# Pool mixer, the next half layer's norm, three plain tiles and the first Strassen tile as one list of steps

## The chip, the cores and the metric

The kernel runs on one core of one Trainium2 chip. The metric is the device time of one execution in microseconds (us). Five engines of the core appear: PE (matrix multiply, with its weight loads shown as PEld), DVE (vector), ACT (scalar), POOL (GpSimd) and SP, which here only issues DMA transfers. Each engine works through its own instructions in order, and semaphores make one wait for another.

## The reference, cut to what matters

One step of a two-layer decoder on 512 prompt rows and 8 sample rows of width 1024. Each layer has two half layers of SwiGLU feed-forward with 2816 hidden columns and a mixer between them. Layer 0 mixes by causal pooling over windows of 2, 4, 8 and 16 rows, one window for each group of 256 columns; layer 1 by windowed attention with sinks.

```
for l in range(DEPTH):
    x = x + 0.5 * _swiglu(_rmsnorm(x, norm_g[l, 0]), ...)   # ffn 0 for l = 0
    h = _rmsnorm(x, norm_g[l, 1])
    if l < N_A_LAYERS:                                      # l = 0
        out, nbuf = _pool_mixer(h, pool_bufs[l], ...)       # (mean over the window - h) @ pool_w * scale
    else: ...                                               # attention
    x = x + out
    x = x + 0.5 * _swiglu(_rmsnorm(x, norm_g[l, 2]), ...)   # ffn 1 for l = 0
```

All of it is float32. `nbuf`, the last 15 mixer inputs, is an output too.

## The kernel before, in words

**Layout.** x is kept transposed: eight tiles `x[0..7]` of 128 columns of the model by 520 tokens (512 prompt, 8 sample). A float32 product is made of three matmuls on pairs: a high part and a low part of each operand (`xh`, `xl`; `wh`, `wl`), high by high, low by high, high by low. ACT makes the high part of a weight piece (L192), DVE the low part (L193). Raw weights come in chunks through SP's queue (L359) into three buffers.

**A half layer** (`ffn`, L683) makes 22 hidden tiles of 128 columns in parts of 8, 8 and 6, and adds each part's down-projection to x. A *plain* tile takes 96 matmuls of 260 columns (L519). A *Strassen* tile takes seven products of twelve matmuls (L545), 84 in all, and needs sums of blocks of x (`t1` to `t4`, L661 to L667, made once in a half layer) and sums of weight blocks, which POOL starts as accumulating DMAs (L156, L157) and DVE finishes (L162, L166). The first `NPL[fi]` tiles of half layer `fi` are plain, because the sums of x are not there yet; before, ffn 1 has two.

**Between ffn 0 and ffn 1.** The last down-projection gives x[0] to x[7] one after the other: u = result times R (L711), x updated (L712), its pair (L348, L349), its square added to `acc` (L468, L472). Then the mixer: `zt` multiplies the token blocks by `pool_w` (L1029, four groups of five blocks of six matmuls); the norm's sums are taken by ten small matmuls over `acc` (L483), the root by twelve small DVE operations (L491 to L498); the products are scaled by the root and split (`zt_evac`); `band` applies the window as a banded matrix, eleven matmuls of 256 columns and two of 8 for each m (L1054, L1062, L1063), and DVE adds the result to x, the 8 sample columns (L1064) apart from the 512 others (L1067). `hx` (L1077), turned by PE (L1097), is the last inputs' output. Then ffn 1 starts: its norm runs between the plain tiles' matmuls, and the sums of x are hooks called between them.

**Order.** Here the instructions of an engine stand in the order of the code, except that a scheduler may move some that are not kept (`later` keeps one). A class `Steps` (L237) exists and is used elsewhere: each step has an engine, a cost, a due time, the steps it must follow and the buffers it takes; `order` plays the engines forward and always starts the earliest-due step that is ready, and `emit` writes the instructions in that order.

SP's queue behind the chunks of weights holds, before ffn 1, one copy for the pooling state (L1107), two for the key and value windows (L1110), one load `sraw` (L1114) and sixteen of 64 bytes for `sink_s` (L1116); the loaded values are negated on DVE (L1147, L1149).

## Time and profile before

| | us |
|---|---|
| three timed runs, median | 1671.43 |
| lowest, highest | 1669.02, 1675.51 |
| the profiled execution | 1674.94 |
| its span in the trace | 1673.1 |
| PE busy | 1647.5 |
| DVE busy | 1254.4 |
| ACT busy | 884.6 |
| POOL busy | 175.2 |

A span reaches from the first to the last traced instruction. Matmul durations overlap, so PE's pace is read from the distance of two starts, or from a piece of the chain of waits with its count. Mean granted clock of PE over the span: 0.992 of full speed. In the prediction, "m6" and "m7" are the last two blocks of the down-projection of ffn 0, "z" the L1029 matmuls, "bands" the L1054 to L1063 matmuls, and times within the span are given as they stand in the trace of before.

### The profile page before, as it was taken

The page shows a single profiled execution, that of the slowest core. Times are in us where ns is not written, and L with a number is a line of the kernel's source. Part 1 is how long each engine was busy: PE and PEld are TensorE (multiplying, and loading weights), DVE is VectorE, ACT ScalarE, POOL GpSimd, SP SyncE. Part 2 cuts the span into 40 slices and gives each one's busy share as a digit, 9 for nine tenths or more (in the row PEclk, how much of TensorE's full clock was granted, in tenths as well). Part 3 has the DMA queues.
Part 4 walks back from the last instruction along what each step waited for, and adds up shares of the span by engine and source line. Part 5 has one row for each costly group of instructions (what it writes and reads, how often), then busy time and mean ns, then how long its engine had stood idle before and what let it go on. Part 6 is the DMA issues. An engine that isn't in the chain of part 4 may idle for free.

```text
span 1673.1 us, 34561 instructions
## 1 busy us (share of the span) xinstructions
PE 1647.5 (98%) x13802; PEld 1629.3 (97%) x13802; DVE 1254.4 (75%) x2400; ACT 884.6 (53%) x1763; POOL 175.2 (10%) x235
## 2 busy tenths in 40 slices
PE   9999999999899999999999999999999999999997
PEld 9999999999899999999999999999989999999997
DVE  7966866887785785878785785778987785785785
ACT  6643643656662562556562562555875663463463
POOL 1101101000101101100201110100220110110100
PEclk9999999999999999999999999999999999999999
DMA  9546846753466665633666666654142565675641
GB/s 241 133 132 135 182 132 136 175 161 97 93 162 152 139 162 145 142 108 114 154 157 156 135 154 162 139 147 113 27 102 71 112 160 143 141 171 137 141 115 52
DMA packets 318240, 227.08 MB, mean 136 GB/s; under 512 B 9568, under 2 KB 293336, under 8 KB 318038
## 3 DMA queue, kind: packets, MB, share of 16 engines
q1 hardware_dynamic: 291360, 178.50, 38.4%
q0 software_dynamic: 23392, 41.83, 15.5%
q10 hardware_dynamic: 3326, 4.53, 0.9%
q8 instruction: 108, 1.77, 0.4%
q14 instruction: 54, 0.44, 0.1%
HBM read 180.89 MB, written 5.04 MB: 111 GB/s over the span
## 4 chain that ended last, share of the span: by engine, by line
PE 93%; DVE 4%; ACT 1%; DMA 1%; issue 1%; DVEq 0%; ACTq 0%
PE ps L545 47%; PE ps L519 32%; PE pa L519 5%; PE ps L1780 2%; PE p L519 1%; PE pb L1385 1%; PE pc L1456 1%; PE ps L1029 1%; PE pc L1441 1%; DMA pr<-in_bands_dram 1%; PE ps L1054 1%; DVE wl L193 1%; PE ps L483 0%; PE t L809 0%; ACT wh L192 0%
## 5 line engine op out<-in xcount | busy, mean ns | idle before, releaser
L192 ACT ACTIVATE wh<-raw 128x512 fp32r<-128x512 f32 (+1 forms) x690 | 418.1, 622 | 511.4 <-PE ps L519 294.2
L193 DVE TENSOR_TENSOR wl<-raw,wh 128x512 fp32r<-128x512 f32 (+1 forms) x690 | 456.6, 677 | 193.1 <-ACT wh L192 189.5
L545 PE MATMUL ps<-th,wh 128*128 128x260 f32 x1264 | 358.5, 284 | 3.6 <-ACT th L345 1.7
L545 PE MATMUL ps<-tl,wh 128*128 128x260 f32 x1264 | 358.1, 284 | 0.6 <-DVE tl L346 0.6
L545 PE MATMUL ps<-th,wl 128*128 128x260 f32 x1264 | 356.4, 284 | 0.8 <-DVE wl L193 0.8
L545 PEld LDWEIGHTS ps<-th,wh 128*128 128x128 f32 x1264 | 238.9, 189 | 5.0 <-ACT th L345 2.1
L545 PEld LDWEIGHTS ps<-tl,wh 128*128 128x128 f32 x1264 | 239.3, 189 | 1.0 <-DVE tl L346 1.0
L545 PEld LDWEIGHTS ps<-th,wl 128*128 128x128 f32 x1264 | 238.4, 189 | 1.2 <-DVE wl L193 1.2
L519 PE MATMUL ps<-hh,wh 128*128 128x260 f32 x1024 | 206.6, 283 | 0.6 <-ACT vtok L1207 0.6
L519 PE MATMUL ps<-hl,wh 128*128 128x260 f32 x1024 | 207.1, 282 | 0.0
L519 PE MATMUL ps<-hh,wl 128*128 128x260 f32 x1024 | 205.1, 282 | 0.0
L545 PE MATMUL ps<-xh,wh 128*128 128x260 f32 x708 | 199.1, 284 | 2.0 <-ACT wh L192 1.5
L545 PE MATMUL ps<-xl,wh 128*128 128x260 f32 x708 | 198.7, 283 | 0.0
L157 POOL DMA_DIRECT2D raw<-raw x79 | 68.4, 866 | 1241.7 <-DVE wl L193 566.5
L545 PE MATMUL ps<-xh,wl 128*128 128x260 f32 x708 | 195.3, 283 | 1.4 <-DVE wl L193 1.4
L519 PEld LDWEIGHTS ps<-hl,wh 128*128 128x128 f32 x1024 | 158.4, 188 | 0.0
L519 PEld LDWEIGHTS ps<-hh,wh 128*128 128x128 f32 x1024 | 157.0, 188 | 1.0 <-ACT vtok L1207 0.9
L519 PEld LDWEIGHTS ps<-hh,wl 128*128 128x128 f32 x1024 | 157.4, 188 | 0.0
L545 PEld LDWEIGHTS ps<-xh,wh 128*128 128x128 f32 x708 | 133.7, 189 | 2.7 <-ACT wh L192 1.9
L711 DVE TENSOR_TENSOR u<-ps,R 128x520 f32<-128x520 f32 x88 | 61.3, 697 | 97.1 <-PE ps L519 97.1
L545 PEld LDWEIGHTS ps<-xl,wh 128*128 128x128 f32 x708 | 133.8, 189 | 0.0
L545 PEld LDWEIGHTS ps<-xh,wl 128*128 128x128 f32 x708 | 131.8, 189 | 1.8 <-DVE wl L193 1.8
(299 smaller groups left out, 3247.1 us busy)
## 6 DMA issues: line engine op xcount, KB each, us to landing
raw<-in_ffn_w_gate_dram SPq DMA_DIRECT2D x87, 512.0 KB
raw<-in_ffn_w_up_dram SPq DMA_DIRECT2D x87, 512.0 KB
raw<-in_ffn_w_down_dram SPq DMA_DIRECT2D x32, 1024.0 KB
S<-in_ffn_w_up_dram SPq DMA_DIRECT2D x79, 256.0 KB
raw<-raw POOLq DMA_DIRECT2D x79, 256.0 KB, 3.3
S<-raw POOLq DMA_DIRECT2D x79, 256.0 KB, 4.6
raw<-in_ffn_w_down_dram SPq DMA_DIRECT2D x16, 768.0 KB
raw<-in_w_q_dram SPq DMA_DIRECT2D x8, 512.0 KB
```

The source lines that it names most:

```text
L157: G.dma_start(blk(raw, 2, 1), blk(raw, 1, 1), accum_op=ALU.add)
L192: nc.scalar.activation(dh, src, AF.Copy)
L193: nc.vector.tensor_tensor(dl, src, dh.bitcast(F32), op=ALU.subtract)
L519: T.matmul(banks[:, hf, :H], a[:, kk, :], hcols(b, hf), start=(first and i == 0), stop=(last and i == 2),)
L545: T.matmul(bank[:, :H], a[:, kk, :], b, start=(not more and kk == 0 and i == 0), stop=(kk == 3 and i == 2), skip_group_check=more,)
L711: V.tensor_tensor(halves(u), banks[m][:, :, :H], halves(R), op=ALU.mult)
L1029: T.matmul(o, a[:, s], b[:, kk, :], start=(n == 0), stop=(n == 5))
L1054: T.matmul(po[:, half * 256 : half * 256 + 256], z[:, tau, c], b, start=(i == 0), stop=(i == len(lst) - 1),)
L1385: T.matmul(o, q_[rows_, qc], k_[rows_, kc_], start=(i == 0), stop=(i == 2))
L1441: T.transpose(pt[:, o : o + P], vals["sm", t, h, bi][:, e, kt * P : (kt + 1) * P], ident)
L1456: T.matmul(po[rows_, bi * P : (bi + 1) * P], vtok[:, max(b - 1, 0) + kt, v0 : v0 + 64], vals["pp", t, h, bi][:, kt * 256 + e * P : kt * 25 ...
L1780: T.matmul(bank, a[:, k % 3, :], b[:, c0:c1], start=(k == 0 and i == 0), stop=(k == 5 and i == 2))
```

## The change

`NPL` becomes (3, 3, 2, 2): ffn 1 has three plain tiles and one Strassen tile fewer. The last down-projection of ffn 0 stops after m = 5; its blocks m6 and m7, the mixer, its norm, ffn 1's norm, three plain tiles and the first six products of the first Strassen tile with the sums of x become one `Steps` list, which sets the order on PE, DVE, ACT and POOL. Further:

- The mixer's norm takes two matmuls for each block, one over `acc` (seven squares) and one over the last square; on PE these run as 20 instead of 10.
- Both norms' roots are one `pow` on POOL instead of the twelve operations on DVE.
- A band's result lies in columns 256 to 776 of a double bank, so that one DVE operation of 520 columns adds it to x.
- `hx` is copied before the norm is known, in pieces kept by the list; the first weight pieces of ffn 1 and the accumulating DMAs are steps too.
- The state, key and value copies, `sraw` and the sink loads are issued by SP one chunk of weights earlier.

```diff
-NPL = (3, 2, 2, 2)
+NPL = (3, 3, 2, 2)
...
-        ffn(0, tmp, mov0, first_hooks(), tt, HH, deferred(1, tmp, "g", XX, mov1, TW), pool_prep(), first_tile)
-
-    with tc.tile_pool(name="pm", bufs=2) as pm:
...
+        hs0 = ffn(0, tmp, mov0, first_hooks(), tt, HH, deferred(1, tmp, "g", XX, mov1, TW), pool_prep(), first_tile, stop=6)
+
+    movk, mov2, tt = [], [], {}
+    later(nc.sync.dma_start(pool_sample[0, :, 0:14, :], state_pool[0, :, 1:15, :]))
...
+    later(nc.sync.dma_start(sraw, attn_sinks.broadcast_to([P, 16])))
+    for b in range(16):
+        later(nc.sync.dma_start(sink_s[b * 8 : (b + 1) * 8, 4:6], attn_sinks.rearrange("l (g r) -> r (l g)", g=2)))
+    with ff_pool() as tmp:
+        first = W.ng
+        have = W.ns - first
+        st = Steps(dict(d=4, w=6, sb=4, sa=2, g=2, t=2, sq=2))
...
+        def norm_sums():
+            vals["f", 0] = f = duo()
+            for t in range(5):
+                lo = t * P if t < 4 else 400
+                o = f[:, 1, t : t + 1]
+                T.matmul(o, acc[:, lo : lo + P], ones[:, 0:1], start=True, stop=False)
+                T.matmul(o, vals["q", 1, 7][:, lo : lo + P], ones[:, 0:1], start=False, stop=True)
...
+        def norm_root():
+            nc.gpsimd.tensor_tensor(r_tok[:, :5], v, minus_half, op=ALU.pow)
...
+        def band(m, part):
...
+            if part == 0:
+                vals["b", m] = duo().rearrange("p a c -> p (a c)")
...
+            o = vals["b", m][:, 256 * part + 256 : min(256 * part + 512, 256 + TOK)]
...
-                V.scalar_tensor_tensor(
-                    x[m][:, SP:], pso[:, :NS], gcol(N_PS, m), x[m][:, SP:], op0=ALU.mult, op1=ALU.add
-                )
-                V.scalar_tensor_tensor(
-                    x[m][:, :SP], po, gcol(N_PS, m), x[m][:, :SP], op0=ALU.mult, op1=ALU.add
-                )
...
+        def x_out(m):
+            V.scalar_tensor_tensor(
+                x[m], vals["b", m][:, 256 : 256 + TOK], gcol(N_PS, m), x[m], op0=ALU.mult, op1=ALU.add
+            )
...
+        def mixed(hs):
+            out_hs.append(hs)
+            with tc.manual_schedule(
+                engines={mybir.EngineType.PE, mybir.EngineType.DVE, mybir.EngineType.Activation, mybir.EngineType.Pool}
+            ):
+                st.emit()
+            begun(1, 4)
+            return NP + 1
+
+        ffn(1, tmp, mov2, [], tt, HH, deferred(N_KV, tmp, "g", XX, movk), given=mixed)
```

**How the instructions move, place 1:** DVE at the end of ffn 0 (`x_82` is x[6], `x_83` x[7]; `raw_4505`, `raw_4645` and `raw_4651` are weight chunks of ffn 1's first tiles). Before:

```order
L193 TENSOR_TENSOR wl<-raw_4505,wh 128x512 [waits PE_49,Activation_49]
L711 TENSOR_TENSOR u<-ps_4817,R 128x520 [waits PE_49]
L349 SCALAR_TENSOR_TENSOR xl<-x_81,gT,xh 128x520 [waits Activation_49]
...
L349 SCALAR_TENSOR_TENSOR xl<-x_82,gT,xh 128x520 [waits Activation_49]
L711 TENSOR_TENSOR u<-ps_4818,R 128x520 [waits PE_49]
L472 TENSOR_TENSOR acc<-acc,sq 128x520 [waits Activation_49]
L346 TENSOR_TENSOR xl<-sts,xh 128x8 [waits Activation_49]
L193 TENSOR_TENSOR wl<-raw_4645,wh 128x512 [waits DMAHW2_49,Activation_49]
L712 SCALAR_TENSOR_TENSOR x_83<-u,x_83 128x520 [waits DVE_49]
L349 SCALAR_TENSOR_TENSOR xl<-x_83,gT,xh 128x520 [waits Activation_49]
```

After:

```order
L1308 TENSOR_TENSOR u<-ps_4874,R 128x520 [waits DVE_49,PE_49]
L1311 SCALAR_TENSOR_TENSOR x_82<-u,x_82 128x520 [waits DVE_49]
L225 TENSOR_TENSOR wl<-raw_4505,wh 128x512 [waits DMAHW6_49,Activation_49]
L1319 SCALAR_TENSOR_TENSOR xl<-x_82,gT,xh 128x520 [waits Activation_49]
L1337 TENSOR_TENSOR acc<-acc,sq 128x520 [waits Activation_49]
L1326 TENSOR_TENSOR xl<-sts,xh 128x8 [waits Activation_49]
L225 TENSOR_TENSOR wl<-raw_4505,wh 128x512 [waits Activation_49]
L1308 TENSOR_TENSOR u<-ps_4920,R 128x520 [waits PE_49]
L1311 SCALAR_TENSOR_TENSOR x_83<-u,x_83 128x520 [waits DVE_49]
L225 TENSOR_TENSOR wl<-raw_4505,wh 128x512 [waits Activation_49]
L1319 SCALAR_TENSOR_TENSOR xl<-x_83,gT,xh 128x520 [waits DVE_49,Activation_49]
```

The update of x[7] now stands right behind its u; before, three operations stood between them. The last square is no longer added to `acc` on DVE.

**Place 2:** SP behind the third chunk of ffn 1's weights. Before:

```order
L359 DMA raw_4770<-in_ffn_w_up_dram 128x8x128 [waits DMAHW4_49]
L359 DMA raw_4907<-in_ffn_w_gate_dram 128x8x128 [waits DMAHW6_49,DMAHW5_49,DVE_49]
L359 DMA raw_4907<-in_ffn_w_up_dram 128x8x128
L359 DMA S<-in_ffn_w_up_dram 128x4x128 [waits DMAHW7_49]
L1107 DMA out_dram<-in_state_pool_dram 8x14336 [waits DMAHW0_49]
```

After:

```order
L368 DMA raw_4796<-in_ffn_w_up_dram 128x8x128 [waits DMAHW4_49]
L1261 DMA out_dram<-in_state_pool_dram 8x14336 [waits DMAHW5_49]
L1264 DMA out_dram<-in_cache_k_win_dram 8x2x16256 [waits DMAHW6_49]
L1264 DMA out_dram<-in_cache_v_win_dram 8x2x16256 [waits DMAHW7_49]
L1268 DMA sraw<-in_attn_sinks_dram 128x16 [waits DMAHW0_49]
L1270 DMA sink_s<-in_attn_sinks_dram 8x2x1 [waits DMAHW1_49]
```

The copies and the small loads now stand ahead of the fourth chunk. The DVE operations that read the small loads (L1563 and L1565, formerly L1147 and L1149) move too, though the diff does not touch them. They now stand in the middle of the mixer's norm and its scaled products (L1350 is the mean, L1356 the fifth block's factor, L1392 the low parts of z); DVE after:

```order
L1326 TENSOR_TENSOR xl<-sts,xh 128x8 [waits Activation_49]
L1563 TENSOR_SCALAR nsinks<-sraw 128x8 [waits DMAHW0_49]
L1563 TENSOR_SCALAR nsinks<-sraw 128x8
L225 TENSOR_TENSOR wl<-raw_4651,wh 128x512 [waits DMAHW1_49,Activation_49]
L1350 TENSOR_SCALAR nv<-ps_5020 128x5 [waits PE_49]
L225 TENSOR_TENSOR wl<-raw_4651,wh 128x512 [waits DMAHW2_49,Activation_49]
L1356 TENSOR_SCALAR r_4869<-r_tok,sel 128x1 [waits Pool_49]
L1392 SCALAR_TENSOR_TENSOR hl<-ps_4974,r_tok,hh 128x256 [waits Activation_49]
L1392 SCALAR_TENSOR_TENSOR hl<-ps_4974,r_tok,hh 128x256 x3
L1565 TENSOR_SCALAR sink_s<-sink_s 128x2 [waits DMAHW4_49,DMAHW5_49,DMAHW3_49,DMAHW6_49,DMAHW2_49,DMAHW7_49,DMAHW1_49,DMAHW0_49]
L1565 TENSOR_SCALAR sink_s<-sink_s 128x2
L1392 SCALAR_TENSOR_TENSOR hl<-ps_5013,r_tok,hh 128x256 [waits Activation_49]
```

Before, they stood among the sums of x, 37 and 50 rows behind the last low part of z.

**Place 3:** DVE at the first Strassen tile (`t_...` are the sums of x, `tl` their low parts, `g` and `hl` a plain tile's result). Before:

```order
L193 TENSOR_TENSOR wl<-raw_4907,wh 128x512 [waits PE_49,Activation_49]
L561 TENSOR_TENSOR hl<-g,hh 128x520 [waits Activation_49]
L661 TENSOR_TENSOR t_5729<-xa 128x260
L662 SCALAR_TENSOR_TENSOR t_5729<-t_5729,xb 128x260 [waits DVE_49]
L667 SCALAR_TENSOR_TENSOR t_5730<-t_5729,xb 128x260 [waits DVE_49]
L346 TENSOR_TENSOR tl<-t_5729,th 128x520 [waits Activation_49]
L666 TENSOR_TENSOR t_5730<-xb,xa 128x260
L162 TENSOR_TENSOR raw_4907<-raw_4907,S 128x512 [waits DMASW2_49,DMASW1_49]
```

After:

```order
L163 TENSOR_TENSOR raw_5045<-raw_5045,S 128x512 [waits DMASW6_49]
L848 TENSOR_TENSOR tl<-t_5709,th 128x520
L848 TENSOR_TENSOR tl<-t_5636,th 128x520
L225 TENSOR_TENSOR wl<-raw_5045,wh 128x512 [waits PE_49,Activation_49]
L848 TENSOR_TENSOR tl<-t_5722,th 128x520
L225 TENSOR_TENSOR wl<-raw_5045,wh 128x512 [waits PE_49,Activation_49]
L167 TENSOR_TENSOR raw_5045<-raw_5045 128x512 [waits DVE_49]
L871 TENSOR_TENSOR g<-ps_5727,R 128x520 [waits PE_49]
```

Before, sums of x were still made behind the second plain tile's low part. Now all sums and their low parts stand ahead of the operation that evacuates the third plain tile's gate (`g<-ps_5727`).

## The prediction

> **What bounds the kernel now.** I read the busy shares and the chain of waits on the page first.

> ```profile
> PE 1647.5 (98%) x13802; PEld 1629.3 (97%) x13802; DVE 1254.4 (75%) x2400; ACT 884.6 (53%) x1763; POOL 175.2 (10%) x235
> PE 93%; DVE 4%; ACT 1%; DMA 1%; issue 1%; DVEq 0%; ACTq 0%
> ```

> PE sets the end nearly everywhere, so only two things can be gained: places where PE waits or runs slowly, and matmuls left out. The change touches one stretch, from m7 to the first Strassen tiles. A table by stage shows where PE loses time in it.

> ```profile
> core 0: us, PE busy (x) PEld busy (x) DVE busy (x) ACT busy (x) POOL busy (x), PEclk, DMA share, GB/s
> 371.00:378.20 7.20, 3.85 (x33) 3.65 (x31) 6.32 (x11) 3.18 (x7) 0.00 (x0) 1.00 0.97 261
> 378.20:385.60 7.40, 7.34 (x36) 7.37 (x37) 4.05 (x17) 4.24 (x13) 1.72 (x2) 0.54 0.73 252
> 385.60:408.40 22.80, 21.46 (x179) 20.75 (x177) 16.28 (x37) 13.26 (x26) 1.07 (x2) 1.00 0.14 38
> 408.40:435.90 27.50, 27.50 (x231) 27.45 (x231) 24.05 (x56) 18.16 (x32) 3.70 (x5) 1.00 0.41 89
> 435.90:446.50 10.60, 5.63 (x32) 4.01 (x30) 8.75 (x18) 6.37 (x13) 0.00 (x0) 1.00 0.01 2
> 446.50:450.40 3.90, 3.86 (x19) 3.87 (x20) 2.56 (x5) 2.74 (x7) 0.00 (x0) 0.56 0.25 75
> 450.40:497.00 46.60, 46.60 (x391) 46.60 (x390) 40.20 (x70) 28.07 (x54) 5.22 (x6) 1.00 0.66 158
> ```

> Four rows are not full: an idle piece before 378.2, two pieces at about half the granted clock (0.54, 0.56), and 435.9 to 446.5, where PE is busy 5.63 of 10.60. The waits of PE from 371 to 450 name the causes:

> ```profile
> PE ps L483 <- DVE acc L472: 3.4, 1, 3.4
> PE ps L545 <- ACT th L345: 1.7, 2, 1.0
> PE ps L1054 <- DVE x L1067: 1.1, 1, 1.1
> PE ps L545 <- DVE wl L193: 1.1, 2, 0.8
> ```

> The norm's sums wait for the last square, one band for a bank that DVE has not read, the first Strassen products for sums of x and weight halves. PE's paces come from pieces of the chain:

> ```profile
> 148.11 74.77 PE ps L545 x624
> 391.20 1.39 PE ps L1054 x11
> 408.49 11.64 PE ps L519 x96
> 420.13 1.01 PE ps L483 x10
> 427.12 0.89 PE ps L504 x8
> 446.54 50.65 PE ps L545 x408
> ```

> A Strassen matmul costs 74.77/624 = 0.1198, a Strassen tile of 84 so 10.06, a plain tile 11.64, ten norm matmuls 1.01, the spread of the root 0.89. A band of thirteen matmuls I take at 1.39 + 0.11 = 1.5. The z matmuls are priced by PE's own timeline:

> ```profile
> 371.14 0.29 PE L1029 MATMUL ps<-th,xh 128*128 128x256 f32 x1
> 374.57 0.28 PE L1029 MATMUL ps<-th,xl 128*128 128x256 f32 x1
> 378.26 1.86 PE L483 MATMUL ps<-ones,acc 128*128 128x1 f32 x10 [3.42 <-DVE acc L472]
> 384.82 0.41 PE L1029 MATMUL ps<-tl,xh 128*128 128x256 f32 x1
> 385.04 0.41 PE L1029 MATMUL ps<-th,xl 128*128 128x256 f32 x1
> ```

> Thirty z lie between 371.14 and 374.7, 0.118 each; at 385 the distance is 0.22.

> **The front: m7 to the first plain tile.** Before, this takes 408.49 - 371.14 = 37.35: z of 3.57, a gap of 3.57, sums 1.0, the other 90 z 10.7, bands 12.0, transposes 1.0, and 3.4 lost to the half clock (two stretches of 3.4 at half speed). That is 35.2; the other 2.1 are the 1.1 wait for a bank and small restarts of PE between bands.

> *The gap.* What the sums wait for is this, before:

> ```profile
> 373.37 0.69 DVE L711 TENSOR_TENSOR u<-ps,R 128x520 f32<-128x520 f32 x1
> 375.26 0.69 DVE L712 SCALAR_TENSOR_TENSOR x<-u,x 128x520 f32<-128x520 f32 x1
> 376.62 0.62 ACT L468 ACTIVATE sq<-x 128x520 f32<-128x520 f32 x1
> 377.43 0.69 DVE L472 TENSOR_TENSOR acc<-acc,sq 128x520 f32<-128x520 f32 x1
> 378.15 2.39 ACT L1077 ACTIVATE hx<-x,gT 128x120 f32<-128x120 f32 x8 [0.91 <-DVE acc L472]
> ```

> After, x[7] follows its u at once, the square comes ahead of the pair's high part, and no addition follows. With u at 373.37, the square would be done at 373.37 + 0.61 + 0.69 + 0.62 and a hand-over, 375.4: a gap of 0.7. But six copies of `hx`, 0.3 each, now stand on ACT ahead of the high halves of the weights, and DVE has the low halves of these ahead of u. I follow it through: squares of m5 added 369.9 (`hx` lies in a square's old buffer and waits for that), `hx` to 371.7, three weight halves and m6's pair and square to about 374.9, u 375.05, x 376.4, square 377.1. The gap is 377.1 - 374.7 = 2.4; between 0.7 and 3.6. Gain 1.15. The second ten norm matmuls take 1.0 of it back.

> *The clock.* In after, PE is idle 2.4 and then has 2.0 of one-column matmuls. The trace has two half-speed stretches: 6.8 long behind an idle of 3.42 and ten such matmuls, and 3.4 long behind the half-empty row 435.9 to 446.5. So the loss is between one stretch (1.7) and two (3.4), or nothing; I take 2.2, nearer one, since this pause is shorter than the first. Gain 1.2. [...]

> *Bands.* Four double banks rotate in the list, and a band's result leaves by one operation of 520 columns; a read over two banks at 520 columns is the L711 row, 0.69. This and the order remove the 2.1, less 0.3 that I leave for restarts: gain 1.8.

> *The hold on DVE.* The readers of `sraw` and `sink_s` now stand in the middle of this, and these loads are late in the trace:

> ```profile
> 363.09 0.57 SPq L359 DMA_DIRECT2D raw<-in_ffn_w_up_dram  x1
> 374.26 0.85 SPq L1107 DMA_DIRECT2D out_dram<-in_state_pool_dram  x1
> 377.09 19.71 SPq L1116 DMA_DIRECT2D sink_s<-in_attn_sinks_dram  x16
> SPq L1116 <- DMA out_dram<-in_cache_v_win_dram: 5.0, 1, 5.0
> SPq L1116 <- DMA sraw<-in_attn_sinks_dram: 1.0, 1, 1.0
> ```

> SP waited for the value copy and then 1.0 more for `sraw`, which by the order of its sixteen issues I put near 392.8, 18.5 after the first copy's issue; the last sink load was issued at 396.5 and I put its landing at 398.5, 24.2 after. In after the copies follow the row at 363.09, so from 363.7: `sraw` at about 382, the sinks at about 388. Behind the first wait stands the norm's mean, behind the second the low parts of z1 and z2. PE, done with the sums at 379.1, has 54 z for banks that are free, with the slow clock to 387.7, and 24 more in z0's banks, to 390.6. The root then comes from POOL:

> ```profile
> 380.16 0.16 DVE L491 TENSOR_SCALAR nv<-ps 128x5 f32<-128x5 f32 x1 [2.04 <-PE ps L483]
> 382.37 0.17 DVE L498 SCALAR_TENSOR_TENSOR r_tok<-nt,ny 128x5 f32<-128x5 f32 x1
> L1853 POOL TENSOR_TENSOR r_tok<-nv,minus_half 128x2 f32<-128x2 f32 x2 | 1.8, 894 | 69.0 <-DVE nv L1847 69.0
> ```

> 0.9 and two hand-overs against 2.4 on DVE. Mean at 383.2, root 384.6, z0's low parts 387; the sinks' wait to 388; z1's five low parts to 390.2, ahead of 390.6. So both waits are just hidden, the second up to 388.6; each microsecond beyond costs one. I allow 0.5.

> The plain tile thus starts at 374.7 + 2.4 + 2.0 + 10.7 + 12.0 + 1.0 + 2.2 + 0.3 = 405.3, against 408.5: a gain of 3.2, before the 0.5.

> **The back: plain tiles to Strassen.** From the first plain tile to where both programs run the same again, before has two plain tiles, the norm (1.01 + 0.89) and 456 Strassen matmuls (the last 408 are the chain's last row) and ends at 446.54 + 50.65 = 497.2. After has three and 372. The count at full pace is 34.9 + 1.9 + 44.6 = 81.4, so 405.3 becomes 486.7: a gain of 10.5. In parts: 3.2 from the front; the third plain tile for a Strassen tile costs 11.64 - 10.06 = 1.6; the 32 matmuls of the half-empty row need 3.8 and took 10.60, 6.8 lost; the next row's 19 need 2.3 of 3.90, 1.6 lost; some 0.5 is spread over the rest. All of this is back if PE finds sums and weights ready. The eleven more microseconds of plain work are the cover: the sums of x before were late by single waits of about 1, and the row 371 to 497 stages sum to 102.2 of DVE work in 126. After has less, by two roots and eight small additions, so about 100 in 116, 86%; in the last stage, where PE never waits, DVE is busy 40.20 of 46.60, 86% too. Were the cover gone, at most the 8.4 comes back. I leave another 0.3 here. POOL's accumulating DMAs stand behind both roots and the four output DMAs, but the first is wanted only at 442.

> **The sum.** 10.5 - 0.5 - 0.3 = 9.7. The profiled execution took 1674.94, 1.84 more than its span and 3.5 more than the median of the runs; a stretch shorter by 9.7 gives 1665.2 by it, and 1671.43 - 9.7 = **1661.7** by the median, which I forecast.

> **The rivals.** *The front gives nothing* (27 in 100): the gap stays 3.6 or the mean is held past 383, and two slow stretches follow. The list has twice the sums, and DVE's wait for `sraw` is new; against it, x[7] is really three operations earlier. The plain tile starts at 408.4 and the time is 1661.7 + 3.1 = 1664.8. *No slow clock in the front* (12): the first slow stretch of the trace followed an idle of 3.42, and 2.4 is shorter; against it, the second followed no single long one. It gives 2.2, of which about 1 is lost again because z3 finds z0's banks unread until 387: 1660.5. *The list starves the Strassen tile* (10): its costs are fixed numbers, and an engine that runs in another rhythm keeps the written order; the 8.4 of the back returns, 1670.1. For it speaks DVE's 86%, against it that sums and low parts stand ahead of the third gate's evacuation. *DVE is held by the sink loads* (6), the slower side: sixteen 64-byte loads behind two copies, with z's low parts and every band behind their wait. It decides from 388.6 on, takes the whole gain at 398.3, and makes the kernel slower by 0.5% from 406.7, which is 43 after the issue instead of 24. The copies then have to compete with more than before: at 18 more than I expect, 1680.

> **How the numbers follow.** My forecast holds with 45 in 100, its own spread 1659.5 to 1663. Half a per cent, 8.4 us, is about what this measurement can tell from no change. Faster by more are the forecast and the case without slow clock, 0.57; within it the front that gives nothing and the starved list, 0.37; slower the held DVE, 0.06. The range, 1656 to 1668.5, takes in the front's bounds (a gap of 0.7 and no slow clock below, nothing gained and a microsecond or two of hold above) and leaves out the starved list and the held DVE.

> **What would show it.** In the profile of after: idle before the norm's sums near 2.4 (L1346); one to two half-clock stretches behind it; DVE's waits at L1563 and L1565, ending by about 382 and 388; the first plain tile (L530 behind the last band) at 405; no idle and no slow clock at the first Strassen products (L556), and these beginning at 442. A wait of PE on `hl` (L1392) would mean the hold; a wait on `th`, `tl` or `wl` at L556 the starved list. My number is wrong if the gain of the back is not there, since it is two thirds of the sum.

## The result and the profile after

The changed kernel takes 1660.49 us (median of 5 runs, 1658.78 to 1662.04) against 1671.43 of the kernel before (5 runs beside them, 1667.08 to 1675.51): a ratio of 0.9941, with a 95% interval of 0.9923 to 0.996. Measured again it was 1661.94 against 1668.49, 0.9955 (0.9942 to 0.9969). It is faster by 6.5 to 11 us; 1661.7 was forecast. One execution of experiment 2 took 3577.46 us and is left out: the median of its five others is 1656.67, while expectations written after it use 1657.3, the median with it.

The page of the profile after, and the table by stage (same columns as before), with the cuts at the first z matmul, the sums, the other z, the bands, the first plain tile and the first Strassen tile:

```profile
PE 1642.4 (99%) x13824; PEld 1626.6 (98%) x13824; DVE 1243.3 (75%) x2361; ACT 879.0 (53%) x1755; POOL 177.4 (11%) x236
```

```profile
370.89:374.45 3.56, 3.56 (x32) 3.56 (x31) 3.53 (x7) 2.31 (x6) 0.00 (x0) 1.00 0.38 153
374.45:377.65 3.20, 2.45 (x23) 2.37 (x22) 1.74 (x4) 2.68 (x6) 0.00 (x0) 1.00 0.39 163
377.65:381.80 4.15, 4.15 (x23) 4.15 (x24) 1.51 (x5) 0.00 (x0) 1.16 (x1) 0.59 0.04 3
381.80:390.11 8.31, 8.31 (x71) 8.20 (x70) 6.09 (x17) 6.42 (x17) 0.41 (x1) 1.00 0.49 128
390.11:403.04 12.93, 12.88 (x113) 12.82 (x112) 11.98 (x21) 10.22 (x18) 2.15 (x4) 1.00 0.04 9
403.04:439.95 36.91, 36.91 (x312) 36.91 (x310) 29.64 (x55) 21.96 (x38) 6.58 (x7) 1.00 0.59 129
439.95:449.95 10.00, 10.00 (x86) 10.00 (x85) 5.86 (x9) 5.52 (x11) 0.00 (x0) 1.00 0.24 69
```

Of the four rows that were not full before, two remain, both short: a pause in the second, and one stretch at about half clock in the third. The last row, the first Strassen products, is full; its counterpart was busy 5.63 of 10.60. From 360 to 450 the list of PE's waits has one line:

```profile
PE ps L1347 <- ACT sq L1330: 0.7, 1, 0.7
```

I cut every trace at the same four events of PE: first z matmul, first plain tile, first Strassen matmul, and the first matmul behind the block of Strassen matmuls, up to which both programs do the same work in sum, but for a plain tile in place of a Strassen tile. The distances, from PE's own timeline; "rest" reaches from the last of these events to the end of the span:

| kernel | front (z to plain) | plain tiles | Strassen | sum | rest |
|---|---|---|---|---|---|
| before | 37.2 | 25.4 | 63.3 | 125.9 | 1176.1 |
| before, again | 36.9 | 25.4 | 63.5 | 125.9 | 1173.2 |
| changed | 32.1 | 36.9 | 44.5 | 113.6 | 1175.2 |
| changed, again | 36.7 | 36.9 | 44.5 | 118.1 | 1175.3 |

So the back (plain tiles and Strassen) gives 88.7 - 81.4 = 7.3 in both profiles, and the front 5.1 in one and about 0.4 in the other. The rest, in which the programs do the same work, varies from 1171.9 to 1176.7 over all profiles here without an order by kernel; this is why I argue from the stretch, and use whole times only with their intervals. The experiments are cut in the same way.

### The profile page after: what moved, and what is told of

It reads as the page before. It is cut to its first block, busy times and chain, and to the rows that moved or that the text cites. A ratio compares the mean times of both kernels' runs of the same rounds, so it can differ in the third digit from the quotient of the medians.

```text
span 1659.6 us, 34553 instructions
## 1 busy us (share of the span) xinstructions
PE 1642.4 (99%) x13824; PEld 1626.6 (98%) x13824; DVE 1243.3 (75%) x2361; ACT 879.0 (53%) x1755; POOL 177.4 (11%) x236
## 4 chain that ended last, share of the span: by engine, by line
PE 94%; DVE 3%; ACT 1%; DMA 1%; issue 0%; SPq 0%; DVEq 0%; ACTq 0%
PE ps L556 47%; PE ps L530 33%; PE pa L530 5%; PE ps L2196 2%; PE pb L1801 1%; PE p L530 1%; PE pc L1872 1%; PE pc L1857 1%; PE ps L1375 1%; PE ps L1412 1%; DMA pr<-in_bands_dram 1%; DVE wl L196 0%; DMA raw<-in_ffn_w_gate_dram 0%; DVE wl L225 0%; DVE xl L358 0%
## 5 line engine op out<-in xcount | busy, mean ns | idle before, releaser
L195 ACT ACTIVATE wh<-raw 128x512 fp32r<-128x512 f32 (+1 forms) x669 | 405.4, 622 | 498.0 <-PE ps L530 291.5
L196 DVE TENSOR_TENSOR wl<-raw,wh 128x512 fp32r<-128x512 f32 (+1 forms) x669 | 442.4, 677 | 184.6 <-ACT wh L195 181.2
L556 PE MATMUL ps<-th,wh 128*128 128x260 f32 x1248 | 353.1, 283 | 1.4 <-DVE sb L649 0.8
L556 PE MATMUL ps<-tl,wh 128*128 128x260 f32 x1248 | 353.1, 283 | 0.0
L556 PE MATMUL ps<-th,wl 128*128 128x260 f32 x1248 | 351.5, 283 | 0.0
L556 PEld LDWEIGHTS ps<-th,wh 128*128 128x128 f32 x1248 | 235.4, 189 | 2.2 <-ACT wh L195 1.2
L556 PEld LDWEIGHTS ps<-tl,wh 128*128 128x128 f32 x1248 | 235.6, 189 | 0.1
L556 PEld LDWEIGHTS ps<-th,wl 128*128 128x128 f32 x1248 | 234.8, 189 | 0.2 <-DVE wl L196 0.2
L530 PE MATMUL ps<-hh,wh 128*128 128x260 f32 x1024 | 206.5, 283 | 0.6 <-ACT vtok L1623 0.6
L530 PE MATMUL ps<-hl,wh 128*128 128x260 f32 x1024 | 207.1, 282 | 0.0
L530 PE MATMUL ps<-hh,wl 128*128 128x260 f32 x1024 | 205.1, 282 | 0.0
L556 PE MATMUL ps<-xh,wh 128*128 128x260 f32 x696 | 195.6, 283 | 0.9 <-ACT sb L639 0.6
L556 PE MATMUL ps<-xl,wh 128*128 128x260 f32 x696 | 195.4, 283 | 0.0
L556 PE MATMUL ps<-xh,wl 128*128 128x260 f32 x696 | 192.1, 282 | 1.0 <-DVE wl L196 1.0
L530 PEld LDWEIGHTS ps<-hl,wh 128*128 128x128 f32 x1024 | 158.3, 188 | 0.0
L530 PEld LDWEIGHTS ps<-hh,wh 128*128 128x128 f32 x1024 | 157.1, 188 | 0.9 <-ACT vtok L1623 0.9
L530 PEld LDWEIGHTS ps<-hh,wl 128*128 128x128 f32 x1024 | 157.4, 188 | 0.0
L556 PEld LDWEIGHTS ps<-xh,wh 128*128 128x128 f32 x696 | 131.3, 189 | 1.3 <-ACT sb L639 0.8
L556 PEld LDWEIGHTS ps<-xl,wh 128*128 128x128 f32 x696 | 131.4, 189 | 0.0
L556 PEld LDWEIGHTS ps<-xh,wl 128*128 128x128 f32 x696 | 129.7, 189 | 1.3 <-DVE wl L196 1.3
```

The costliest lines, as they stand in the source:

```text
L195: nc.scalar.activation(dh, src, AF.Copy)
L196: nc.vector.tensor_tensor(dl, src, dh.bitcast(F32), op=ALU.subtract)
L530: T.matmul(banks[:, hf, :H], a[:, kk, :], hcols(b, hf), start=(first and i == 0), stop=(last and i == 2),)
L556: T.matmul(bank[:, :H], a[:, kk, :], b, start=(not more and kk == 0 and i == 0), stop=(kk == 3 and i == 2), skip_group_check=more,)
```

## The experiments

**1. The third plain tile alone.** The prediction gave the back's gain to the cover of eleven more microseconds of plain work. The kernel before with one number changed:

```diff
-NPL = (3, 2, 2, 2)
+NPL = (3, 3, 2, 2)
```

> The kernel before with a single number changed: three plain tiles in ffn 1 instead of two (one Strassen tile fewer), no list of steps. If the third plain tile alone is the cover for the sums of x (my theory), the idle stretch and the slow clock at the first Strassen products go, the gap before the norm's sums (3.4) stays, and the time is 1671.4 - 8.4 + 1.6 = about 1664.5. If the list is needed for it (rival), PE still waits 5 to 8 at the first Strassen products and the time is 1671 to 1673.

Measured: 1671.27 against 1670.06, ratio 1.0012 (1.0002 to 1.0022). The cover gives nothing: plain 37.0 and Strassen 52.8, 89.7 together against 88.7 before. (The front, 35.5, is 1.7 shorter: 3.4 at half clock follow the sums here, not 6.8.) PE's waits at the first Strassen products, and DVE's waits at that place:

```profile
PE ps L545 <- ACT th L345: 2.2, 1, 2.2
PE ps L545 <- DVE tl L346: 1.4, 1, 1.4
PE ps L545 <- DVE wl L193: 0.8, 1, 0.8
```

```profile
DVE g L602 <- PE ps L519: 5.9, 2, 5.5
DVE g L604 <- ACT wh L192: 1.7, 1, 1.7
```

DVE's timeline shows what these 5.5 are:

```profile
434.56 1.31 DVE L561 TENSOR_TENSOR hl<-g,hh 128x520 fp32r<-128x520 f32 x2 [0.31 <-ACT hh L559]
441.41 0.70 DVE L602 TENSOR_TENSOR g<-ps,R 128x520 f32<-128x520 f32 x1 [5.54 <-PE ps L519]
442.02 0.68 DVE L162 TENSOR_TENSOR raw<-raw,S 128x512 f32<-128x512 f32 x1
```

The evacuation of the third tile's gate (L602) stands ahead of the Strassen tile's weight sums and of half the sums of x. DVE comes to it when PE is in the middle of that tile, stands idle for 5.5 (ACT for 7.1 behind it), and everything that was meant to be done under the third tile is still to do when the tile ends. An engine that works in written order can't use cover that its own order puts behind the cover's result.

**2. The list with two plain tiles.** The same number the other way, in the changed kernel:

```diff
-NPL = (3, 3, 2, 2)
+NPL = (3, 2, 2, 2)
```

> The changed kernel with two plain tiles in ffn 1 again, the list kept. Cover theory: Strassen starts 11.6 earlier, finds sums of x late, PE idles and slows there by 5 to 8, and the tile saved gives 1.6 back: 1664 to 1667. Rival (the list's order alone closes the gaps): no idle at the first Strassen products and 1659.

Measured: 1656.67 against 1670.06, 0.9929 (0.9914 to 0.9944). The rival holds. The chain of this kernel:

```profile
405.82 10.15 PE ps L530 x84
420.97 10.20 PE ps L530 x84
431.17 54.84 PE ps L556 x456
```

456 Strassen matmuls run in one piece at 0.1203, with no wait, and start 25.3 behind the first plain tile instead of 36.9. Plain 25.3 and Strassen 54.8 make 80.2: 8.5 less than before, and 1.2 less than the changed kernel. So the list is what closes the gaps, the third plain tile adds nothing to it, and its price is 1.2 (two plain tiles with the readers late, experiment 7, give 80.7, with a wait of 0.3 in the fifth Strassen tile; with the old norm end, experiment 8, 80.1). It does so by its order, not by less work: from 408 to 434 DVE is busy 22.4 of 26 before and 22.7 here, but the sums of x start on DVE at 410.4 and the last at 428.2, ahead of the first Strassen matmul at 431.0; before, they start at 423.9 and the last at 445.1, with the first Strassen matmul at 433.7, and in experiment 1 at 422.7 and 454.0, with it at 444.1.

Of what came with the list, the norm's end, the readers of the small loads and the single additions do not move the back (experiments 3, 6 and 11: 81.4 each); the root on POOL and the weight pieces as steps were not taken apart from the order. A list with one plain tile was not run.

**3. The norm's end as before.** In the changed kernel the last square is again added on DVE behind the pair's high part, the sums are ten matmuls, and `hx` comes behind the last addition:

```diff
-                T.matmul(o, acc[:, lo : lo + P], ones[:, 0:1], start=True, stop=False)
-                T.matmul(o, vals["q", 1, 7][:, lo : lo + P], ones[:, 0:1], start=False, stop=True)
+                T.matmul(o, acc[:, lo : lo + P], ones[:, 0:1], start=True, stop=True)
...
+                add("a7", "DVE", 0.7, d + 0.3, lambda: sum_of(1, 7), after=["q7", "a6"], reads=[("sq", "q7")])
```

> The changed kernel with the norm's end as before: last square behind the pair's high part, added on DVE, ten matmuls for the sums instead of twenty, the copies of hx behind the last addition. Theory: the gap before the sums grows from 0.75 to about 2.4, the sums shrink from 2.2 to 1.0, so the first plain tile starts 0.4 to 0.8 later, 1661 to 1662; if the longer pause brings a second slow stretch, 1.7 more. Rival (the order at m7 is what the front gained): the gap returns to 3.4 with two slow stretches, the plain tile 3 to 4 later, 1664.

Measured: 1660.54 against 1670.06, 0.995 (0.9938 to 0.9962); front 32.2. The later sums cost nothing, because the list puts twelve more z matmuls ahead of them. PE waits at another place, and the chain says for what:

```profile
PE ps L1372 <- DVE nv L1347: 1.7, 1, 1.7
```

```profile
363.54 15.26 DMA sraw<-in_attn_sinks_dram
```

The mean stands on DVE behind the negation of `sraw`, whose load landed at 378.8; PE, ahead with its z matmuls, stood for it.

**4. The small loads made late.** Their tiles are cleared on DVE behind the mean, so the loads have to follow, and their readers are kept between the low parts of z0 and z1:

```diff
+        def clear():
+            V.memset(sraw, 0.0)
+            V.memset(sink_s[:, 4:6], 0.0)
+
+        add("clear", "DVE", 0.1, 11.1, clear, after=["nm"])
+        add("small", "-", 0.0, -60.0, small, after=["clear"])
+        add("neg", "DVE", 0.4, E_DUE[0] + 3.6, negate, after=["small", "ez03"])
```

> The changed kernel with the small loads (sraw and sixteen of sink_s) made late: they are issued behind the next chunk of weights and only after the norm's mean, and their readers stay between the low parts of z0 and of z1. I expect the last to land at 390 to 392, DVE to stand from about 383 to then, and PE to wait for z1's banks (wanted at about 388.6, two microseconds of DVE work behind the wait): 3.5 to 5.5 of idle, the first plain tile that much later, 1664 to 1666, and 1.7 more if the idle slows the clock. If a wait of DVE at this place is off the path (rival), the plain tile starts at 403 as now and the time is 1660.5.

Measured: 1664.17 against 1670.06, 0.9963 (0.995 to 0.9976), 2 to 4 us above the changed kernel's two medians, but with an interval that overlaps its second one; the trace has to decide. DVE stood 5.6 and PE 2.5 for the low parts behind it:

```profile
DVE sink_s L1528 <- DMA sink_s<-in_attn_sinks_dram: 5.6, 1, 5.6
```

```profile
PE ps L1372 <- DVE hl L1389: 2.5, 1, 2.5
PE ps L1344 <- ACT sq L1327: 2.3, 1, 2.3
```

The last sink load landed at 390.5 (387.77 + 2.69 in its chain), PE wanted z1's banks at 390.5 and had them at 393.0, after DVE's five low parts. So DVE's wait is on the path once the last load lands later than about 388 (390.5 less the 2.5 of low parts); the prediction had 388.6. Behind PE's idle the clock is at half from 393.1 to 396.5, which costs 1.5 more (16 z matmuls start there 0.213 apart, against 0.118 at whole clock), and the front is 37.7. The idle was 1 below the range I gave, since PE came to that point late itself: this profile has the 2.3 at the sums as well (experiment 12). That each microsecond past 388 costs one is worked out, not shown: there is one point.

**5. The kernel before again.**

> The kernel before, profiled a second time, to see which of its losses come back in every execution. Theory: the gap of 3.4 before the norm's sums, two slow stretches behind it, the 1.1 wait at a band and 5 to 7 of waits at the first Strassen products are in the written order and are all there again, within 0.5 each. Rival: they belong to that one execution (which was 3.5 above the median), and half of them or more are gone.

Measured: 1671.49, one run. All four losses are there again, the waits at the first Strassen products with 4.3 after 5.0 (up to 450), and the stretch is 125.9 in both profiles:

```profile
PE ps L483 <- DVE acc L472: 3.2, 1, 3.2
PE ps L545 <- ACT th L345: 1.7, 2, 1.0
PE ps L1054 <- DVE x L1067: 1.1, 1, 1.1
```

The two spans differ by 3.4; 2.9 of it lie in the rest, 1176.1 against 1173.2, and none in the stretch.

**6 and 7. The readers of the small loads behind ffn 1,** once with three plain tiles and once with two:

```diff
-            V.tensor_scalar(s4[:, g], sr[:, g], -1.0, None, op0=ALU.mult)
+            later(V.tensor_scalar(s4[:, g], sr[:, g], -1.0, None, op0=ALU.mult))
```

(and the same for `sink_s`).

> The changed kernel with the readers of sraw and sink_s kept at their place in the code, behind ffn 1, so that DVE waits for no small load in the mixer. If both waits are hidden behind z matmuls (prediction), PE's times do not move: 1660.5, plain tile at 403 to 405. If the hold costs (rival), the mean comes 2 to 2.7 earlier and the kernel gains 1 to 2: 1658.5 to 1659.5.

> The list with two plain tiles, and the readers of the small loads kept behind ffn 1. Hidden hold: same as the list with two plain tiles, 1657.3. Costly hold: 1655.5 to 1656.5.

Measured: 1661.76 against 1670.56, 0.9951 (0.9938 to 0.9963), front 32.1; and 1660.13, 0.9936 (0.9924 to 0.9949), front 33.6. With twenty matmuls the hold on DVE is hidden, as predicted: the front is 32.1 with it and without it. The front of 33.6 has a wait as short, 0.9, but 6.8 at half clock behind it instead of 3.4. The second time is above that of experiment 2; its stretch is 114.3 against 115.7 there, and its rest 2.5 longer (1175.1 against 1172.6), in work that is the same. The intervals of experiments 2 and 7 overlap, so these two kernels can't be told apart by time.

**8. Two plain tiles, readers late and the norm's end as before,** the edits of 2, 6 and 3 together.

> The list with two plain tiles, the readers of the small loads kept behind ffn 1, and the norm's end as before (last square added on DVE, ten matmuls, twelve more z matmuls ahead of them). With the norm's end as before and three plain tiles, PE did not wait for the sums at all, but 1.7 for the mean, which stood behind the wait for sraw. Without that wait I expect no idle of PE in the front and at most one slow stretch: 1.5 to 3 less than the list with two plain tiles, 1654.5 to 1656. If the mean is not what PE waits for (rival), 1657.3.

Measured: 1653.61 against 1670.56, 0.9904 (0.9889 to 0.9919). This beats both kernels. Its chain:

```profile
375.78 1.25 PE ps L1344 x10
377.03 9.41 PE ps L1372 x78
399.52 10.15 PE ps L530 x84
```

and its table at the norm:

```profile
375.03:376.90 1.87, 1.40 (x14) 1.23 (x12) 1.28 (x3) 1.87 (x7) 0.00 (x0) 1.00 0.00 0
376.90:386.40 9.50, 9.50 (x82) 9.42 (x82) 6.11 (x16) 7.20 (x20) 1.20 (x1) 1.00 0.44 111
```

The clock stays at 1.00 behind the sums: the front is 29.2, 2.9 less than in the changed kernel's better profile. The time came out 1 below the range expected, since I had still reckoned with a slow stretch; this profile's rest, 1171.9, is also the shortest of all.

**9. The same with three plain tiles,** against experiment 3 a change of the readers alone.

> Three plain tiles, the norm's end as before (ten matmuls, last square added on DVE), and the readers of the small loads behind ffn 1: against the old norm end alone, only the readers move. If DVE's wait for sraw is what PE's 1.7 and the slow stretch behind it came from, the front (first z to first plain tile) falls from 32.2 to about 29.2, the whole stretch from 113.6 to 110.6 and the time from 1660.5 to 1655 to 1657. If the readers are without effect (rival, as they were with twenty matmuls), front 32.2 and 1660.5.

Measured: 1656.6 against 1669.86, 0.9921 (0.9908 to 0.9934), against 0.995 with the readers early. Front 28.8, sum 110.2, both as expected. With ten matmuls the hold is not hidden and costs 3.4 of front: 1.7 of wait, and one slow stretch of 3.4 behind it. And against experiment 8 the third plain tile costs 36.9 + 44.5 - 80.1 = 1.3 in the trace.

**10. The twenty small matmuls in five pieces,** six z matmuls between two pieces, readers late, three plain tiles:

```diff
+        between = ("z10", "z11", "z12", "z13", "z04")
+        for t in range(5):
+            add(
+                f"ns{t}", "PE", 0.45, 10.5 + 0.1 * t, lambda t=t: norm_sums(t), after=["q7", "a6", between[t]],
```

> Three plain tiles, readers late, and the norm's twenty small matmuls kept, but in five pieces of four with six z matmuls between two pieces, so that PE never has 2.2 of one-column matmuls in a row. If the slow stretch comes from a pause of PE in which one-column matmuls count like idle time, it is gone, and the front falls from 32.1 to about 30, or less what PE then waits for z0's banks since the mean is later by 3: 30 to 32, 1658.5 to 1661. If the idle of 0.75 alone brings it (rival), it stays, and the front is 32 or more.

Measured: 1662.57 against 1669.86, 0.9964 (0.9951 to 0.9977); front 32.6. Time and front lie above the ranges, by 1.6 and 0.6. The slow stretch behind the sums is gone, as the theory has it (in the one profile there is), and what PE loses instead is idle time:

```profile
PE ps L1377 <- DVE hl L1394: 2.0, 1, 2.0
PE ps L1349 <- ACT sq L1330: 0.6, 1, 0.6
```

```profile
373.50:379.50 6.00, 5.38 (x48) 5.30 (x47) 2.90 (x6) 2.69 (x6) 0.00 (x0) 1.00 0.24 89
379.50:382.80 3.30, 3.30 (x30) 3.30 (x29) 0.44 (x2) 1.08 (x3) 1.20 (x1) 1.00 0.13 31
382.80:385.10 2.30, 0.29 (x3) 0.08 (x2) 1.66 (x4) 2.30 (x8) 0.00 (x0) 1.00 1.18 322
385.10:390.00 4.90, 4.90 (x42) 4.90 (x42) 4.01 (x10) 3.45 (x11) 0.00 (x0) 1.00 0.19 45
```

The clock is whole throughout, behind the wait of 2.0 too, but the mean comes later by the z matmuls between the pieces, and PE waits for z0's low parts. The front adds up: the 28.8 of experiment 9, ten more small matmuls at 1.1, and waits of 0.6 and 2.0. It has a floor that the chain from last square to z0's low parts sets; spreading the sums lengthens this chain. The nine timed executions fall in two groups, 1660.25 to 1662.57 and 1666.13 to 1667.01; the profile is of the first, and what the others did is not known.

**11. Two additions for each band,** 8 and 512 columns, in the changed kernel:

```diff
-                x[m], vals["b", m][:, 256 : 256 + TOK], gcol(N_PS, m), x[m], op0=ALU.mult, op1=ALU.add
+                x[m][:, SP:], vals["b", m][:, 256 + SP : 256 + TOK], gcol(N_PS, m), x[m][:, SP:], op0=ALU.mult, op1=ALU.add
...
+                x[m][:, :SP], vals["b", m][:, 256 : 256 + SP], gcol(N_PS, m), x[m][:, :SP], op0=ALU.mult, op1=ALU.add
```

> The changed kernel with each band's result added to x by two DVE operations, 8 and 512 columns, instead of one of 520 over two banks. Eight operations of 0.15 more on DVE, in a stage in which PE waits for nothing: PE's times stay (bands 13.07, first plain tile at 403 to 405, 1660.5). If the single operation is needed to keep DVE ahead of PE (rival), PE waits at bands or at the first plain tile by up to 1.2.

Measured: 1661.38 against 1669.86, 0.9953 (0.9939 to 0.9968). One wait of 0.2 at a band is new; the time is the changed kernel's. One operation over two banks takes 750 ns (before 743 and 223) and is worth nothing here that can be measured. The front, 35.3, is longer by the 2.3 at the sums and by 6.8 at half clock behind it instead of 3.4, not by the bands.

**12. The changed kernel again.**

> The changed kernel once more. In the profiles so far ACT waited for the loads of the bands, 30 us ahead of the mixer, either 2.5 to 2.9 or 3.9 to 4.4 in all, and the front of a list kernel with twenty small matmuls was 32.1 to 33.6 in the first case and 35.3 to 35.5 in the second. If the landing of these loads moves the front (theory), this profile falls in one of the two pairs: waits below 3 with a gap of 0.75 to 0.9, or about 4.2 with a gap of 2.3. If gap and loads are unrelated (rival), it can show one of each. Time in both cases 1659 to 1662, the back (first plain tile to the last common Strassen matmul) 81.4.

Measured: 1661.94 against 1668.49, 0.9955. ACT's waits for the loads of the bands, of this profile, of the changed kernel's first one, and of the kernel before:

```profile
ACT G L1246 <- DMA pr<-in_bands_dram: 4.8, 4, 2.0
```

```profile
ACT G L1246 <- DMA pr<-in_bands_dram: 2.9, 4, 2.0
```

```profile
ACT G L994 <- DMA pr<-in_bands_dram: 4.2, 3, 1.9
```

These rows are of the first copies of the bands, and by them the profiles fall in two groups: 2.5 to 2.9 in seven, called early from here on, 3.9 to 4.8 in seven, called late. (A second wait for such loads, L999 or L1251, is 2.9 to 3.3 in all.) Of the list kernels with twenty matmuls in one piece, the four of the late group (experiments 2, 4, 11, 12) waited 2.3 for the last square, the three of the early one (the first profile, 6, 7) 0.7 to 0.9, without an exception. The traces show the way: ACT waits 0.19 for the second of these loads in the first profile of the changed kernel and 1.9 in experiment 4, from there on its operations stand 1.8 to 2.0 later, DVE works off its queue as much later, and with it comes the last square. The update of x[5] starts 5.3 to 5.8 ahead of the first z matmul in the seven early profiles of lists, and 3.5 to 4.0 ahead in the four late ones. No run moves these loads on purpose, so this is followed in the traces, not tested. The clock behind the pause, in this profile:

```profile
373.40:376.50 3.10, 0.60 (x5) 0.34 (x3) 2.97 (x6) 1.52 (x4) 0.00 (x0) 0.86 0.74 317
376.50:380.70 4.20, 4.18 (x19) 4.18 (x20) 1.50 (x5) 2.02 (x5) 0.00 (x0) 0.50 0.07 17
380.70:386.00 5.30, 5.30 (x27) 5.30 (x27) 2.88 (x10) 1.57 (x4) 1.57 (x1) 0.51 0.24 62
```

The clock is at half for 10.2 us, 9.4 of them with PE at work, against 3.4 in the first profile. The front is 36.7, over the 35.3 to 35.5 that I expected for this group, by the longer slow stretch. The length of the pause alone does not set that of the slow stretch: behind the same 2.3 it was 3.4 in experiment 4 and 6.8 in experiments 2 and 11 (last section). What makes the band loads land late is not settled: all three profiles of the order before are in the late group, and four of eleven list kernels.

## Why the prediction was right, and where it was not

**The time** was right: 1660.49 for 1661.7, inside the narrow range of 1659.5 to 1663 too. Faster by more than half a per cent had 0.57; the two measurements give 0.59 and 0.45%, and their intervals reach to both sides. Part of it is luck: for the 9.7 reckoned, the stretch gave 12.3 in the first profile and 7.8 in the second, and the larger share of the sum came about in another way than I gave. By its steps:

**The back, 10.5 less the front's 3.2.** The size held to the tenth, 7.3 in the trace of both profiles. The reason did not, so that the size is luck as far as it rests on the reason. The step that failed is "The eleven more microseconds of plain work are the cover": as a cause it is refuted from both sides, by experiment 1, where the tile brings a loss of 0.1% and leaves the gaps, and by experiment 2, where the gaps are gone without it. DVE's share of 86%, on which I leaned, was not the question, since DVE is as busy in experiment 2 as before; what counted is which operation stands in front on DVE: the sums of x early, and not behind the evacuation of an unfinished tile. The term for the third tile, 1.6, measured 1.2 to 1.3 (experiments 2 and 8), and it is a pure loss.

**The gap.** 2.4, followed by hand through the rows of before, is the 2.3 of the late group; the early group has 0.7 to 0.9. The row of before from which I started belongs to the late group itself, and nothing in one profile told that it could be otherwise. The first profile came out at the lower bound of 0.7 that I had given.

**The second ten norm matmuls,** put at 1.0, were undersized, since I did not join them with the clock. All twenty in one piece, with a pause among them, went with half clock in all seven profiles; with them and the hold removed (experiments 8 and 9) the front is 28.8 to 29.2 and the clock whole.

**The clock,** 2.2 in a range up to 3.4: I had put a stretch of 3.4 at a loss of half of it, 1.7. By the distances of matmuls (256 columns: 0.213 at half clock, 0.118 at whole; one column: 0.213 and 0.112) the loss was 1.5 in the first profile, 16 of 256 columns, and 4.4 in the second, 25 of 256 and 20 of one, past my upper bound. A pause shorter than the 3.42 of before can cost a slow stretch too: here it followed an idle of 0.75 with 2.2 of one-column matmuls behind it, and gaps of 2.3 came with 3.4 to 10.2 at half speed. The last section has them side by side.

**The hold.** `sraw` came at 379.6 instead of 382, in a wait that cost PE nothing:

```profile
379.64 0.24 DVE L1563 TENSOR_SCALAR nsinks<-sraw 128x8 f32<-128x8 f32 x2 [2.73 <-DMA sraw<-in_attn_sinks_dram]
385.43 0.23 DVE L1565 TENSOR_SCALAR sink_s<-sink_s 128x2 f32<-128x2 f32 x2
```

The sinks had landed before DVE came to them at 385.4, where I had a wait to 388. That both are "just hidden" was right with this norm (experiment 6), and the point from which a wait costs was right (experiment 4). The root on POOL took 1.57 instead of 0.9, and the bands with the transposes ran in 13.1 with the waits gone, where I had reckoned 13.3.

**The rivals.** "The front gives nothing" is nearly what the second profile shows, 36.7 for 36.9 to 37.2, with a gap of 2.3, not 3.6, and a longer slow stretch than I had reckoned; in experiments 2 and 11, of the late group too, the front still gives 1.4 to 2. "No slow clock" did not occur with twenty matmuls in one piece. "The list starves the Strassen tile" is wrong in all eleven profiles of lists; PE waits at the first Strassen tile in none of them.

## What to carry to other kernels

Work that is meant to hide something helps only if the engine in question does the hidden part first: before adding cover, look at which operation that engine has in front, and whether it waits for the cover's own result (here 5.5 us of an idle DVE under a tile that was put there for it). A change of several parts should be taken apart even when its sum comes out: the order was worth 8.5 in the back, the third tile cost 1.2, and the better kernel (1653.61, a ratio of 0.9904) has the list, two plain tiles, ten matmuls for the norm and no reader of a late load ahead of the mean. A gap that a hand chain gives from one profile is the gap of that execution; a second profile of the same kernel can show whether it is one of two. The same holds for a slow stretch, which in the changed kernel was 3.4 in one profile and 10.2 in the other: one profile with a whole clock does not show that a pause is free.

## What the runs showed of the hardware

| kernel | idle of PE, us | small matmuls behind or around it | half clock, us |
|---|---|---|---|
| changed; experiment 6 | 0.75; 0.9 | twenty | 3.4; 3.4 |
| experiment 7 | 0.85 | twenty | 6.8 |
| experiment 4 | 2.3 | twenty | 3.4 |
| experiments 2 and 11 | 2.3 | twenty | 6.8 |
| experiment 12 | 2.3 | twenty | 10.2 |
| before; again; experiment 1 | 3.4; 3.2; 3.3 | ten | 6.8; 6.8; 3.4 |
| experiment 8 | 0.5 | ten | none |
| experiment 9 | next to none | ten | none |
| experiment 10, at the sums | 0.6 | twenty in five pieces | none |
| experiment 10, at z0's low parts | 2.0 | none | none |
| experiment 3, at the mean | 1.7 | none | 3.4 |
| experiment 4, at z1's banks | 2.5 | none | 3.4 |

The same wait of 2.3 at the sums thus went with 3.4, 6.8 and 10.2. How much matmul work stands ahead of a slow stretch is an estimate: the columns of the matmuls that start in the 3.41 us before it, at the pace of 0.1198 for 260, where the trace gives the start of the stretch (to about 0.05 in the experiments).

| profile | half clock from | work in the 3.41 us before, us | in each 3.41 us at half clock, us |
|---|---|---|---|
| before | 378.71 | 0.0 | 1.2, 1.9 |
| before | 446.97 | 1.1 | 1.9 |
| changed | 378.42 | 0.8 | 1.9 |
| experiment 2 | 377.4 | 0.0 | 0.5, 1.9 |
| experiment 3 | 380.6 | 1.4 | 1.9 |
| experiment 4 | 379.5 | 0.0 | 1.9 |
| experiment 4 | 393.1 | 0.6 | 1.9 |
| experiment 6 | 378.0 | 1.1 | 1.9 |
| experiment 7 | 375.8 | 0.8 | 1.3, 1.9 |
| experiment 12 | 375.6 | 1.2 | 0.0, 1.2, 1.8 |

Against these, experiment 8 has at least 1.5 in any 3.41 us from 371 to 389, experiment 9 at least 2.0, and the clock is whole there. No limit follows from it: before, the 3.41 us from 440.15 have 1.3 and the whole clock behind them, experiment 3 has half clock behind 1.4, and experiment 10 keeps the whole clock though the 3.41 us from 381.8 have 1.1.

In this count a matmul of one column is next to nothing: in experiment 4 the 3.41 us from 376.05 have 1.4 of idle time and then 2.0 of such matmuls alone, and half clock follows. In experiment 10 the same twenty small matmuls with z matmuls between them left the clock at 1.00 (373.5 to 379.5), and so did PE's wait of 2.0 at z0's low parts.
